# Ordering edits in a planned single-core kernel: state products a step later, PSUM exits by priority, two scan groups per output product, side splits spread out

## The chip, the cores and the metric

The kernel runs on one core of one Trainium2 chip, in one launch. The metric is device time in microseconds (us), the median of several runs; less is better. The engines are named as in the profile: PE is TensorE's matmul, PEld its weight load, DVE is VectorE, ACT is ScalarE, POOL is GpSimd, and SP is SyncE, which here issues nearly all DMAs.

## The reference

One step of a decoder layer in float32, on 1024 prompt tokens and on 8 samples of 8 tokens: a half-weight SwiGLU block, a token mixer of two branches, another half-weight SwiGLU block, and a final RMSNorm. Cut to what matters here:

```python
x = x + 0.5 * swiglu(rmsnorm(x, norm_ffn1), ffn1_w_in, ffn1_w_out)
proj = rmsnorm(x, norm_mix) @ w_in                       # u | z | xbc | dt | two gates
pool = (pool_mix(u) per group @ pool_w_group * pool_scale) @ pool_w_out
xbc  = silu(causal_conv(xbc));  xs, B, C = split(xbc)
per chunk of 128 tokens, per group of 8 heads (4 groups):
    st     = B^T (decay_end * dt * xs)                   # state product
    y      = (C B^T * decay) (dt * xs) + exp(a) * (C h)  # h: state before the chunk
    h      = h * chunk_decay + st
y    = rmsnorm_per_group((y + D * xs) * silu(z)) * ssd_norm
mix  = (gate0 * pool + gate1 * (y @ ssd_w_out)) @ w_o
x = x + mix
x = x + 0.5 * swiglu(rmsnorm(x, norm_ffn2), ffn2_w_in, ffn2_w_out)
return rmsnorm(x), and the new pooling, convolution and scan states
```

D_MODEL is 1024, D_FF 2816, the scan has 32 heads of 64 and a state of 128.

## The kernel before

All matrix products are made as three products of rounded float32 parts: a matrix is split into a high and a low part (`split`, `load_w`: ScalarE makes the high part, VectorE subtracts it), and high by high, low by high and high by low are summed in PSUM (`products`, L319 on). The products of the two feed-forward inputs and of `w_in` also use a Winograd-like scheme of seven products (`wino`). The tokens stand in two halves: half 0 has 512 prompt tokens, half 1 has 512 prompt tokens and the 64 sample tokens (576). An activation is held transposed, 128 channels by tokens, in a pool of 42 shared buffers (`act`); a product of half 0 fills one PSUM bank, one of half 1 two banks of 288 columns.

The stages follow each other: first feed-forward block, input projection (`in_proj`), mixer ("mix"), second feed-forward block. In the mixer the order of dense products is `pool_branch(0)`, `pool_branch(1)`, then for each half the products of `ssd_w_out` group by group (`ssd_out` for groups 0 to 2, `merge` for group 3 and the gates), then `out_proj`. Beside them the scan runs (`scan`, `ssd_group`): half 0, groups 0 to 3, then half 1; each group has 4 chunks (5 in half 1, the last being the samples).

The order is set by a planner in the kernel itself. `pe[0]` is TensorE time as the kernel counts it: each matmul adds its columns over 2400 us (four times that for plain float32). Side work is written as chains, generators that yield a pause in this time; `tick()`, which dense products call after each operand, steps every chain that is due, and `finish(c)` runs one to its end at once. So all pauses end at ticks. Afterwards the framework orders each engine's queue by the place in the program, with a model of its own of what is ready when; `tc.high_priority(n)` moves what stands in it n places ahead.

What the change touches:

- `ssd_group` (L1448 on): for each chunk the loads, a pause of `STEP[h]`, the second part of `ssd_a` (transposes `pxT`, `pcb`; `xdt`, `xd` and `btok` on VectorE and ScalarE; `ab`), a pause, `ssd_b` of the chunk before (`pyo`, `pyd`), then `ssd_st` of this chunk: the state product `pst<-xd,btok`, POOL's product of the old state and VectorE's sum (L1444).
- `gating` (L1482 on): y by z, the norm (`rstd`: `pss`, a power on POOL, then a pause of `R_WAIT0`, then `prb`), and the splits `yhl`, into buffers for two groups; it waits until the products of the group two before are counted in `freed`.
- `ssd_out`, `merge`, `out_proj`, `pool_branch`: the exits from PSUM on VectorE (L1565, L1593, L1609, L1252) have no priority.
- `load_w`: a weight block is loaded raw and split, unless it was split ahead by a side chain and written to DRAM (`part`, `parted`); then its two parts are loaded. `side()` splits ahead blocks of `ffn1_w_out`, `ffn2_w_in`, `w_o` and `pool_w_out` in the first stage, `split_so` those of `ssd_w_out` during `in_proj`. The pauses in `part` are `PART_W` (2.5) and `PART_PACE` (1.5).
- `in_proj` loads four pairs of `d` (`load_d`, high and low part of the pooled difference) ahead of the mixer; `pool_branch` loads the rest. `after1` starts the norm of half 1 (`norm_parts`) at pace 0.5.

Of the kernel before, what the change touches and what calls it, by code (L numbers as in the profile page):

```python
# [12 lines left out]
ALU = mybir.AluOpType  # L13

P = 128
D = 1024
KD = D // P
# [23 lines left out]

PRODUCTS = (("1", 0), ("2", 1), ("6", 0), ("5", 2), ("7", 0), ("3", 2), ("4", 0))

STEP = (5.4, 4.3)
STEP_S = 1.0
POST = 1.0
GP = (1.0, 1.2)
HN_AT, HN_PACE = 25.0, 2.0
MP = 2.0
R_WAIT0 = 2.0  # L50
R_WAIT = 0.5
F_Y = 0.5
X1_AT = 4.0
T_AT, T_PACE = 2.0, 1.5
TURN_AT, CONST_AT = 60.0, 40.0
HP, HP_ST = 40, 0
PART_AT, PART_W, PART_PACE = 6.0, 2.5, 1.5


@with_exitstack  # L60
def tile_hybrid_pool_ssd_macaron(
# [239 lines left out]

    parted, nth = {}, [0]

    def part(w, chunks):

        for k0, nk, c0 in chunks:
            t = fx(name="pr")[:, : nk * P]
            dma(t.rearrange("p (k c) -> p k c", c=P),
                w[k0 * P : (k0 + nk) * P, c0 : c0 + P].rearrange("(k p) c -> p k c", p=P))
            yield PART_W  # L310
            a = fx(F32R, "ph")[:, : nk * P]
            split(t, a, t.bitcast(F32R))
            to = [dp.tile([P, nk * P], F32, tag=nm("part"), name=nm("part")) for _ in range(2)]
            dma(to[0], a.bitcast(F32))
            dma(to[1], t)
            parted[w.tensor.name, k0, c0] = to
            yield PART_PACE

    def products(out, Wh, Wl, kk, cs, xs, k, nk):  # L319
        for ps_, (W, lo_) in enumerate(((Wh, False), (Wh, True), (Wl, False))):  # L320
# [490 lines left out]
    def after1(h, xt):  # L811
        o = []
        if h == 0:
            prep1m[0] = start(norm_parts(xt, 0, i_gm, o, HN_PACE, xnd), HN_AT), o
        for m in range(KD):
            dma(xspill[h][m], xt[m][:, : NTOK[h]])
        if h == 1:
            finish(prep1m[0][0])
            _, hi, lo, _, hl = prep1m[0][1][0]
            xn = [fx(name="xn") if k >= 4 else act((P, 576), name="xn") for k in range(KD)]  # L820
            for k in (0, 4, 1, 5, 2, 6, 3, 7):
                dma(xn[k][:, : NTOK[0]], xnd[k])
            prep1m[0][1][0] = (0, hi, lo, xn, hl)
            prep1m[1] = start(norm_parts(xt, 1, i_gm, o, 0.5), 0.5), o

    def mix_dt(h, xs):

# [299 lines left out]
    def in_proj(prep):  # L1127

        dts = []

        def plain(x):
            h = x[0]
            dts.append(mix_dt(h, [x]))
            for i in range(N_GATE[h]):
                pg = dense(W, 0, KD, OFF_G0 + i * P, [x], name="pg0")[0]
                t = fx(name="t0")
                func(t, pg, h, AF.Tanh, 0.5)
                dma(gd[h][i], t[:, : NTOK[h]])

        X = operands(prep, plain)  # L1140
        both = [(h, X[h]) for h in HALVES]
        last = [False]

        def worker():
            while work or not last[0]:
                if work:
                    yield from work.pop(0)
                else:
                    yield 1.0

        c = poster[0] = start(worker())
        work.append(sample_hist())
        split_so = start(part(ssd_w_out[0], so_chunks), 2.0)
        for i in range(N_GATE[0], 16, 2):
            proj_pair("g", i, i + 1, both)
        for g in range(NG):
            for kind, ia, ib in (("c", 16 + g, 20 + g), ("c", 4 * g, 4 * g + 1), ("c", 4 * g + 2, 4 * g + 3),
                                 ("u", 2 * g, 2 * g + 1), ("z", 4 * g, 4 * g + 1), ("z", 4 * g + 2, 4 * g + 3)):
                proj_pair(kind, ia, ib, both)
        ahead_d = []  # L1160
        for k in range(4):
            ahead_d.append(load_d(0, k))
        for i in range(N_GATE[1], N_GATE[0], 2):
            proj_pair("g", i, i + 1, both[1:])
        last[0] = True
        for c_ in dts + [split_so, c]:
            finish(c_)
        dma(new_pool_s[0, :, 0:7, :], state_pool[0, :, 8:HIST, :])
        return ahead_d
# [31 lines left out]
    def side():  # L1201
        yield from part(ffn1_w_out[0], out01)
        yield from part(ffn2_w_in[0], [(kb, 4, c0 + ff * P) for ff in range(N_PLAIN[0]) for kb in (0, 4) for c0 in (0, FF)])
        for w in (w_o[0], pool_w_out[0]):
            yield from part(w, [(kb, 4, m * P) for m in range(KD) for kb in (0, 4)])

    ffn(wi1, ffn1_w_out[0], prep1, after1, side=side())
    ahead_d = in_proj(prep1m)
# [17 lines left out]
    def pool_branch(h):  # L1226

        N = NTOK[h]
        fh, fl = [None] * KD, [None] * KD
        d = early[h]  # L1230

        def fetch_d(gi):
            for k in (2 * gi, 2 * gi + 1):
                if k not in d:
                    d[k] = load_d(h, k)

        fetch_d(0)
        for gi in range(4):
            if gi < 3:
                fetch_d(gi + 1)  # L1240
            dh, dl = zip(*(d.pop(k) for k in (2 * gi, 2 * gi + 1)))
            for j, pg in enumerate(dense2(wg[gi], 0, 0, [(h, dh, dl)], ("ps", "ps"), name="pgm")):
                m = gi * 2 + j
                fh[m], fl[m] = act((P, N), F32R, "fh"), act((P, N), F32R, "fl")
                for pt, (a, b) in zip(pg[0], PIECES[h]):
                    split(pt[:, : b - a], fh[m][:, a:b], fl[m][:, a:b], cols[:, i_ps + m : i_ps + m + 1])
        for m in range(KD):
            t = act((P, N), name="t0")
            dma(t, gd[h][m])
            pb = dense(pool_w_out[0], 0, KD, m * P, [(h, fh, fl)], name="pbp")[0]  # L1250
            for pt, (a, b) in zip(pb, PIECES[h]):
                V.scalar_tensor_tensor(t[:, a:b], t[:, a:b], 1.0, pt[:, : b - a], op0=ALU.add, op1=ALU.mult)  # L1252
            dma(accd[h][m], t)
            if h == 0 and m in (4, 6):
                early[1][m // 2 - 2] = load_d(1, m // 2 - 2)
# [192 lines left out]
    def ssd_group(h, g, Bf, Cf, xs4, dts, zs):  # L1448
        y4 = xs4
        prev = None  # L1450
        step = STEP[h]
        for c in range(4 + h):
            ga = ssd_a(h, g, c, Bf, Cf, xs4, dts)
            next(ga)
            if c == 3:
                for j in range(4):
                    z = act((P, NTOK[h]), name="z")
                    dma(z, zd[h][g * 4 + j])
                    zs.append(z)
            yield step  # L1460
            try:
                next(ga)
            except StopIteration as e:
                a = e.value
            yield step
            if prev:
                for w in ssd_b(h, g, *prev, Cf, y4, dts):
                    yield w
            prev = (c, a, ssd_st(h, g, c, a, dts))
        yield step  # L1470
        for w in ssd_b(h, g, *prev, Cf, y4, dts):
            yield w
        if h == 1:
            pt = psum("ps", "pfin")
# [76 lines left out]
        finish(gated[h, g][0])  # L1551
        return gated[h, g][1][0]

    def ssd_out(h, g, acc):

        yn = scanned(h, g)
        for m in range(KD):
            pb = dense(ssd_w_out[0], g * 4, 4, m * P, [yn], name="pso")[0]
            if g == 0:
                acc[m] = act((P, NTOK[h]), name="acc2")  # L1560
            for pt, (a, b) in zip(pb, PIECES[h]):
                if g == 0:
                    S.copy(acc[m][:, a:b], pt[:, : b - a])
                else:
                    V.tensor_tensor(acc[m][:, a:b], acc[m][:, a:b], pt[:, : b - a], op=ALU.add)  # L1565
        freed[0] += 1

    def merge(h, acc):

        N = NTOK[h]  # L1570
        t1 = [None] * KD
# [10 lines left out]
                merged[0] += 1  # L1582

        ch = start(head(), MP)
        yn = scanned(h, NG - 1)
        mh, ml = [], []
        for m in range(KD):
            pb = dense(ssd_w_out[0], (NG - 1) * 4, 4, m * P, [yn], name="pso")[0]
            while merged[0] <= m:
                ch.step()  # L1590
            a_, b_ = act((P, N), F32R, "mh"), act((P, N), F32R, "ml")
            for pt, (a, b) in zip(pb, PIECES[h]):
                V.scalar_tensor_tensor(t1[m][:, a:b], t1[m][:, a:b], 1.0, pt[:, : b - a], op0=ALU.add, op1=ALU.mult)  # L1593
            V.tensor_tensor(t1[m], t1[m], acc[m], op=ALU.add)
            split(t1[m], a_, b_, 0.5)
            mh.append(a_)
            ml.append(b_)
        freed[0] += 1
        return mh, ml

    def out_proj(h, mh, ml):
        N = NTOK[h]
        out = []
        for m in range(KD):
            x_ = act((P, N), name="x2")
            dma(x_, xspill[h][m])
            pw = dense(w_o[0], 0, KD, m * P, [(h, mh, ml)], name="pwo")[0]
            for pt, (a, b) in zip(pw, PIECES[h]):
                V.tensor_tensor(x_[:, a:b], x_[:, a:b], pt[:, : b - a], op=ALU.add)  # L1609
            dma(xspill[h][m], x_)  # L1610
            if h == 1:
                out.append(x_)
# [4 lines left out]
        pool_branch(h)  # L1617
    for h in HALVES:
        acc = [None] * KD
        for g in range(NG - 1):  # L1620
            ssd_out(h, g, acc)
        mhl = merge(h, acc)
        if h == 1:
            o = []
            prep2.append((start(norm_parts(reload(0), 0, i_g2, o, 2.0)), o))
# [126 lines left out]
```

## Time and profile before

| | |
|---|---|
| median of 3 runs | 2969.01 us (2965.47 to 2973.89) |
| the profiled execution's own time | 2975.98 us |
| its span, first to last instruction | 2974.2 us |
| mean granted TensorE clock | 0.987 |
| PE busy | 2838.9 us (95%) |
| PEld busy | 2579.6 us (87%) |
| DVE busy | 1763.4 us (59%) |
| ACT busy | 1374.6 us (46%) |
| POOL busy | 989.6 us (33%) |
| DMA moved | 528.96 MB |

How to read it: the profile is one execution. A row of waits says which engine stood before which tile's instruction, what ended it, and then the total in us, how often, and the longest. A window row gives its length, the busy time of PE, PEld, DVE, ACT and POOL with their instructions, the granted TensorE clock, the DMA share and GB/s. An order-of-time row begins with start and duration in us; what stands in brackets is the idle time before it and what ended that. Matmuls are pipelined and their rows overlap: the distance of two starts is what one costs.

### The profile page before, as it was taken

How to read it: one execution, taken by the hardware profiler on the slowest of the kernel's cores; microseconds unless marked ns; L12 is line 12 of the kernel's file. 1: busy time of each engine (PE TensorE's matmuls, PEld its weight loads, DVE VectorE, ACT ScalarE, POOL GpSimd, SP SyncE). 2: the span in 40 equal slices, each digit the busy share in tenths (PEclk: the TensorE clock that was granted, in tenths of full speed). 3: DMA queues.
4: the chain of work that ended last, by engine and by line, in shares of the span. 5: the costliest groups of instructions: out<-in, count | busy, mean ns of one | idle time of the engine just before them, and what ended most of it. 6: DMA issues, size and time to landing. Idle time of an engine off the chain costs nothing. (4 is left out here: it accounts for less than half of the span.)

```text
span 2974.2 us, 51139 instructions
## 1 busy us (share of the span) xinstructions
PE 2838.9 (95%) x18494; PEld 2579.6 (87%) x18494; DVE 1763.4 (59%) x2843; ACT 1374.6 (46%) x3008; POOL 989.6 (33%) x1011
## 2 busy tenths in 40 slices
PE   7999999999999989999989999889999999999998
PEld 6999899789989989998977887678888999997898
DVE  6665655534375696877865657766665544453432
ACT  5444444423345555554545555566333444443422
POOL 5444444100133454555522223322234444440000
PEclk9999999999999999999999999999999999999999
DMA  4677663856346663333368777776765422226652
GB/s 124 199 238 234 200 202 114 270 182 207 111 123 218 217 204 102 125 96 125 104 205 295 259 265 228 256 220 204 234 234 176 150 79 82 84 96 210 210 162 72
DMA packets 535709, 528.96 MB, mean 178 GB/s; under 512 B 38164, under 2 KB 367752, under 8 KB 535448
## 3 DMA queue, kind: packets, MB, share of 16 engines
q1 hardware_dynamic: 535440, 525.70, 55.5%
q8 instruction: 145, 2.38, 0.3%
q14 instruction: 108, 0.88, 0.1%
q10 hardware_dynamic: 16, 0.00, 0.0%
HBM read 374.36 MB, written 151.44 MB: 177 GB/s over the span
## 5 line engine op out<-in xcount | busy, mean ns | idle before, releaser
L162 PE MATMUL pw<-X,wh 128*128 128x288 f32 (+1 forms) x2484 | 623.4, 330 | 11.0 <-ACT v L559 3.5
L162 PE MATMUL pw<-X,wl 128*128 128x288 f32 (+1 forms) x1644 | 472.7, 288 | 4.6 <-DVE wl L443 4.6
L162 PEld LDWEIGHTS pw<-X,wh 128*128 128x128 f32 x2484 | 418.2, 189 | 49.9 <-ACT v L559 4.1
L162 PE MATMUL pw<-hl,wh 128*128 128x512 f32 x1072 | 391.9, 399 | 9.0 <-DVE t L563 5.2
L162 PE MATMUL pw<-hi,wh 128*128 128x288 f32 x1120 | 332.9, 297 | 4.8 <-ACT t L595 3.6
L162 PE MATMUL pw<-lo,wh 128*128 128x288 f32 x1120 | 331.5, 296 | 0.0
L162 PE MATMUL pw<-hi,wl 128*128 128x288 f32 x1120 | 331.4, 296 | 0.0
L443 DVE TENSOR_TENSOR wl<-s,wh 128x512 fp32r<-128x512 f32 x288 | 220.6, 768 | 179.4 <-ACT wh L442 154.6
L436 POOL TENSOR_TENSOR s<-wraw,wraw 128x512 f32<-128x512 f32 x144 | 204.4, 1420 | 338.3 <-DVE wl L443 226.3
L162 PEld LDWEIGHTS pw<-X,wl 128*128 128x128 f32 x1644 | 310.8, 189 | 5.5 <-DVE wl L443 5.5
L162 PE MATMUL pw<-hl,wl 128*128 128x256 f32 x1072 | 300.2, 280 | 1.9 <-DVE wl L443 1.8
L294 DVE TENSOR_TENSOR wl<-wraw,wh 128x512 fp32r<-128x512 f32 x196 | 136.3, 696 | 246.0 <-ACT wh L293 231.2
L293 ACT ACTIVATE wh<-wraw 128x512 fp32r<-128x512 f32 x196 | 117.8, 603 | 299.5 <-PE po L162 224.5
L162 PEld LDWEIGHTS pw<-hl,wh 128*128 128x128 f32 x1072 | 201.8, 188 | 46.9 <-DVE t L563 6.6
L443 DVE TENSOR_TENSOR wl<-wraw,wh 128x512 fp32r<-128x512 f32 x216 | 169.7, 786 | 121.1 <-ACT wh L442 114.0
L442 ACT ACTIVATE wh<-s 128x512 fp32r<-128x512 f32 x288 | 181.2, 629 | 124.8 <-PE pw L162 121.1
L162 PEld LDWEIGHTS pw<-hi,wh 128*128 128x128 f32 x1120 | 211.7, 189 | 17.7 <-ACT t L595 4.3
L162 PE MATMUL po<-hh,wh 128*128 128x288 f32 (+1 forms) x800 | 211.3, 324 | 4.4 <-ACT hh L354 4.3
L162 PEld LDWEIGHTS pw<-lo,wh 128*128 128x128 f32 x1120 | 211.9, 189 | 0.0
L162 PEld LDWEIGHTS pw<-hi,wl 128*128 128x128 f32 x1120 | 211.9, 189 | 0.0
L162 PE MATMUL po<-hr,wh 128*128 128x288 f32 (+1 forms) x800 | 211.5, 323 | 0.2 <-DVE hr L356 0.2
L162 PE MATMUL po<-hh,wl 128*128 128x288 f32 (+1 forms) x800 | 211.1, 323 | 0.0
(384 smaller groups left out, 6371.8 us busy)
## 6 DMA issues: line engine op xcount, KB each, us to landing
wraw<-in_ffn_w_in_dram SPq DMA_DIRECT2D x188, 256.0 KB
wh<-part SPq DMA_DIRECT2D x188, 256.0 KB
wl<-part SPq DMA_DIRECT2D x188, 256.0 KB
wraw<-in_w_in_dram SPq DMA_DIRECT2D x144, 256.0 KB
wraw<-in_ffn_w_out_dram SPq DMA_DIRECT2D x120, 256.0 KB
part<-ph SPq DMA_DIRECT2D x96, 256.0 KB
part<-pr SPq DMA_DIRECT2D x96, 256.0 KB
ab<-acsd SPq DMA_DIRECT2D x64, 256.0 KB
```

What stands on the lines that cost most here:

```text
L162: T.matmul(out, lhsT, rhs, start=start, stop=stop, skip_group_check=free)
L293: S.activation(wh, raw, AF.Copy)
L294: V.tensor_tensor(wl, raw, wh.bitcast(F32), op=ALU.subtract)
L436: G.tensor_tensor(t, a, b, op=op)
L442: S.activation(wh, a, AF.Copy)
L443: V.tensor_tensor(wl, a, wh.bitcast(F32), op=ALU.subtract)
```

## The change

It does nine things. (1) `ssd_st` of a chunk is called in the next chunk's round, between the two pauses, and after the last pause for the last chunk. (2) `in_proj` loads six pairs of `d` ahead. (3) `R_WAIT0` is 3.5. (4) In half 1 the scan's groups 0 and 1 go into one output product of eight operands (`SETS`), and `freed` counts both at its end. (5) Five exits from PSUM get `high_priority(60)`. (6) `pool_w_out` is no longer split ahead. (7) The side splits start later and pause longer: 20 at first, then 4.0 and 3.0; for `ssd_w_out` 5.0 and 5.0. (8) The norm of half 1 before `in_proj` has pace 1.2. (9) `STEP` is 5.2 and 4.1.

```diff
@@ -41,20 +41,21 @@
 
 PRODUCTS = (("1", 0), ("2", 1), ("6", 0), ("5", 2), ("7", 0), ("3", 2), ("4", 0))
 
-STEP = (5.4, 4.3)
+STEP = (5.2, 4.1)
 STEP_S = 1.0
 POST = 1.0
 GP = (1.0, 1.2)
 HN_AT, HN_PACE = 25.0, 2.0
 MP = 2.0
-R_WAIT0 = 2.0
+R_WAIT0 = 3.5
 R_WAIT = 0.5
 F_Y = 0.5
 X1_AT = 4.0
 T_AT, T_PACE = 2.0, 1.5
 TURN_AT, CONST_AT = 60.0, 40.0
-HP, HP_ST = 40, 0
-PART_AT, PART_W, PART_PACE = 6.0, 2.5, 1.5
+HP, HP_ST, HP_EV = 40, 0, 60
+SETS = (((0,), (1,), (2,), (3,)), ((0, 1), (2,), (3,)))
+PART_AT, PART_W, PART_PACE = 20.0, 4.0, 3.0
 
 
 @with_exitstack
@@ -301,20 +302,20 @@
 
     parted, nth = {}, [0]
 
-    def part(w, chunks):
+    def part(w, chunks, wait=PART_W, pace=PART_PACE):
 
         for k0, nk, c0 in chunks:
             t = fx(name="pr")[:, : nk * P]
             dma(t.rearrange("p (k c) -> p k c", c=P),
                 w[k0 * P : (k0 + nk) * P, c0 : c0 + P].rearrange("(k p) c -> p k c", p=P))
-            yield PART_W
+            yield wait
             a = fx(F32R, "ph")[:, : nk * P]
             split(t, a, t.bitcast(F32R))
             to = [dp.tile([P, nk * P], F32, tag=nm("part"), name=nm("part")) for _ in range(2)]
             dma(to[0], a.bitcast(F32))
             dma(to[1], t)
             parted[w.tensor.name, k0, c0] = to
-            yield PART_PACE
+            yield pace
 
     def products(out, Wh, Wl, kk, cs, xs, k, nk):
         for ps_, (W, lo_) in enumerate(((Wh, False), (Wh, True), (Wl, False))):
@@ -821,7 +822,7 @@
             for k in (0, 4, 1, 5, 2, 6, 3, 7):
                 dma(xn[k][:, : NTOK[0]], xnd[k])
             prep1m[0][1][0] = (0, hi, lo, xn, hl)
-            prep1m[1] = start(norm_parts(xt, 1, i_gm, o, 0.5), 0.5), o
+            prep1m[1] = start(norm_parts(xt, 1, i_gm, o, 1.2), 0.5), o
 
     def mix_dt(h, xs):
 
@@ -1150,7 +1151,7 @@
 
         c = poster[0] = start(worker())
         work.append(sample_hist())
-        split_so = start(part(ssd_w_out[0], so_chunks), 2.0)
+        split_so = start(part(ssd_w_out[0], so_chunks, 5.0, 5.0), 2.0)
         for i in range(N_GATE[0], 16, 2):
             proj_pair("g", i, i + 1, both)
         for g in range(NG):
@@ -1158,7 +1159,7 @@
                                  ("u", 2 * g, 2 * g + 1), ("z", 4 * g, 4 * g + 1), ("z", 4 * g + 2, 4 * g + 3)):
                 proj_pair(kind, ia, ib, both)
         ahead_d = []
-        for k in range(4):
+        for k in range(6):
             ahead_d.append(load_d(0, k))
         for i in range(N_GATE[1], N_GATE[0], 2):
             proj_pair("g", i, i + 1, both[1:])
@@ -1201,8 +1202,7 @@
     def side():
         yield from part(ffn1_w_out[0], out01)
         yield from part(ffn2_w_in[0], [(kb, 4, c0 + ff * P) for ff in range(N_PLAIN[0]) for kb in (0, 4) for c0 in (0, FF)])
-        for w in (w_o[0], pool_w_out[0]):
-            yield from part(w, [(kb, 4, m * P) for m in range(KD) for kb in (0, 4)])
+        yield from part(w_o[0], [(kb, 4, m * P) for m in range(KD) for kb in (0, 4)])
 
     ffn(wi1, ffn1_w_out[0], prep1, after1, side=side())
     ahead_d = in_proj(prep1m)
@@ -1248,8 +1248,9 @@
             t = act((P, N), name="t0")
             dma(t, gd[h][m])
             pb = dense(pool_w_out[0], 0, KD, m * P, [(h, fh, fl)], name="pbp")[0]
-            for pt, (a, b) in zip(pb, PIECES[h]):
-                V.scalar_tensor_tensor(t[:, a:b], t[:, a:b], 1.0, pt[:, : b - a], op0=ALU.add, op1=ALU.mult)
+            with tc.high_priority(HP_EV):
+                for pt, (a, b) in zip(pb, PIECES[h]):
+                    V.scalar_tensor_tensor(t[:, a:b], t[:, a:b], 1.0, pt[:, : b - a], op0=ALU.add, op1=ALU.mult)
             dma(accd[h][m], t)
             if h == 0 and m in (4, 6):
                 early[1][m // 2 - 2] = load_d(1, m // 2 - 2)
@@ -1458,6 +1459,8 @@
                     dma(z, zd[h][g * 4 + j])
                     zs.append(z)
             yield step
+            if prev:
+                prev += (ssd_st(h, g, *prev, dts),)
             try:
                 next(ga)
             except StopIteration as e:
@@ -1466,9 +1469,9 @@
             if prev:
                 for w in ssd_b(h, g, *prev, Cf, y4, dts):
                     yield w
-            prev = (c, a, ssd_st(h, g, c, a, dts))
+            prev = (c, a)
         yield step
-        for w in ssd_b(h, g, *prev, Cf, y4, dts):
+        for w in ssd_b(h, g, *prev, ssd_st(h, g, *prev, dts), Cf, y4, dts):
             yield w
         if h == 1:
             pt = psum("ps", "pfin")
@@ -1551,21 +1554,26 @@
         finish(gated[h, g][0])
         return gated[h, g][1][0]
 
-    def ssd_out(h, g, acc):
-
-        yn = scanned(h, g)
+    def ynorm(h, gs):
+        ys = [scanned(h, g) for g in gs]
+        return h, sum((y[1] for y in ys), []), sum((y[2] for y in ys), [])
+
+    def ssd_out(h, gs, acc):
+
+        yn = ynorm(h, gs)
         for m in range(KD):
-            pb = dense(ssd_w_out[0], g * 4, 4, m * P, [yn], name="pso")[0]
-            if g == 0:
+            pb = dense(ssd_w_out[0], gs[0] * 4, 4 * len(gs), m * P, [yn], name="pso")[0]
+            if gs[0] == 0:
                 acc[m] = act((P, NTOK[h]), name="acc2")
-            for pt, (a, b) in zip(pb, PIECES[h]):
-                if g == 0:
-                    S.copy(acc[m][:, a:b], pt[:, : b - a])
-                else:
-                    V.tensor_tensor(acc[m][:, a:b], acc[m][:, a:b], pt[:, : b - a], op=ALU.add)
-        freed[0] += 1
-
-    def merge(h, acc):
+            with tc.high_priority(HP_EV):
+                for pt, (a, b) in zip(pb, PIECES[h]):
+                    if gs[0] == 0:
+                        S.copy(acc[m][:, a:b], pt[:, : b - a])
+                    else:
+                        V.tensor_tensor(acc[m][:, a:b], acc[m][:, a:b], pt[:, : b - a], op=ALU.add)
+        freed[0] += len(gs)
+
+    def merge(h, gs, acc):
 
         N = NTOK[h]
         t1 = [None] * KD
@@ -1582,20 +1590,21 @@
                 merged[0] += 1
 
         ch = start(head(), MP)
-        yn = scanned(h, NG - 1)
+        yn = ynorm(h, gs)
         mh, ml = [], []
         for m in range(KD):
-            pb = dense(ssd_w_out[0], (NG - 1) * 4, 4, m * P, [yn], name="pso")[0]
+            pb = dense(ssd_w_out[0], gs[0] * 4, 4 * len(gs), m * P, [yn], name="pso")[0]
             while merged[0] <= m:
                 ch.step()
             a_, b_ = act((P, N), F32R, "mh"), act((P, N), F32R, "ml")
-            for pt, (a, b) in zip(pb, PIECES[h]):
-                V.scalar_tensor_tensor(t1[m][:, a:b], t1[m][:, a:b], 1.0, pt[:, : b - a], op0=ALU.add, op1=ALU.mult)
+            with tc.high_priority(HP_EV):
+                for pt, (a, b) in zip(pb, PIECES[h]):
+                    V.scalar_tensor_tensor(t1[m][:, a:b], t1[m][:, a:b], 1.0, pt[:, : b - a], op0=ALU.add, op1=ALU.mult)
             V.tensor_tensor(t1[m], t1[m], acc[m], op=ALU.add)
             split(t1[m], a_, b_, 0.5)
             mh.append(a_)
             ml.append(b_)
-        freed[0] += 1
+        freed[0] += len(gs)
         return mh, ml
 
     def out_proj(h, mh, ml):
@@ -1605,8 +1614,9 @@
             x_ = act((P, N), name="x2")
             dma(x_, xspill[h][m])
             pw = dense(w_o[0], 0, KD, m * P, [(h, mh, ml)], name="pwo")[0]
-            for pt, (a, b) in zip(pw, PIECES[h]):
-                V.tensor_tensor(x_[:, a:b], x_[:, a:b], pt[:, : b - a], op=ALU.add)
+            with tc.high_priority(HP_EV):
+                for pt, (a, b) in zip(pw, PIECES[h]):
+                    V.tensor_tensor(x_[:, a:b], x_[:, a:b], pt[:, : b - a], op=ALU.add)
             dma(xspill[h][m], x_)
             if h == 1:
                 out.append(x_)
@@ -1617,9 +1627,9 @@
         pool_branch(h)
     for h in HALVES:
         acc = [None] * KD
-        for g in range(NG - 1):
-            ssd_out(h, g, acc)
-        mhl = merge(h, acc)
+        for gs in SETS[h][:-1]:
+            ssd_out(h, gs, acc)
+        mhl = merge(h, SETS[h][-1], acc)
         if h == 1:
             o = []
             prep2.append((start(norm_parts(reload(0), 0, i_g2, o, 2.0)), o))
```

## The prediction

> **What bounds the kernel.** I read the page's first part, then the waits of TensorE over the whole span, then the windows around its longest waits, then the order of time on TensorE, VectorE and SyncE there.
>
> ```profile
> span 2974.2 us, 51139 instructions
> ...
> PE 2838.9 (95%) x18494; PEld 2579.6 (87%) x18494; DVE 1763.4 (59%) x2843; ACT 1374.6 (46%) x3008; POOL 989.6 (33%) x1011
> ```
>
> TensorE is busy 2838.9 of 2974.2 us, so 135 us is all that better order can win; the change alters no matmul, only when each is asked for. The execution's own time is 2975.98 us, 1.8 us beside the span and 7 us over the median of the runs (2969.01). I sum savings against this execution and take them off the median.
>
> The waits of TensorE (total us, times, longest us):
>
> ```profile
> PE pst L162 <- DVE xd L1333: 8.1, 4, 5.4
> PE pgm L162 <- DMA d<-dl: 7.8, 1, 7.8
> ...
> PE pw L162 <- DVE t L563: 5.2, 6, 1.6
> PE pg L162 <- DVE wl L294: 4.9, 3, 2.5
> ...
> PE prb L166 <- POOL rsm L362: 4.2, 4, 1.6
> ...
> PE pst L162 <- ACT ab L1343: 3.6, 2, 2.7
> ...
> PE pso L162 <- DVE t L1593: 2.6, 4, 1.1
> PE pso L162 <- DVE acc L1565: 2.3, 2, 1.5
> ...
> PE pbp L162 <- DMA wl<-part: 2.0, 2, 1.1
> PE pwo L162 <- DVE x L1609: 1.9, 1, 1.9
> ```
>
> No wait is large; the change aims at these ten rows, 42.6 us together. A wait also costs afterwards. In windows around three of them the granted clock (the column after POOL's) is low:
>
> ```profile
> 1550.00:1567.00 17.00, 9.17 (x32) 6.96 (x31) 1.70 (x3) 1.38 (x2) 0.64 (x1) 0.70 0.96 339
> 1872.00:1884.00 12.00, 6.55 (x17) 4.28 (x16) 11.20 (x16) 9.01 (x22) 8.01 (x5) 0.72 1.00 339
> 826.00:834.00 8.00, 5.67 (x18) 4.49 (x19) 8.00 (x12) 4.89 (x9) 3.29 (x5) 0.79 0.26 66
> ```
>
> (1-0.70)x17 = 5.1, (1-0.72)x12 = 3.4 and (1-0.79)x8 = 1.7 us of clock are missing, part of it while TensorE stands anyway. The third window's longest wait is 2.5 us, so short waits cost clock too. The Trainium skill, TensorE: Matmul & The Clock Gate, Part 1 (The HAM clock gate), has the clock fall to half after an idle window of about 3.4 us and rise after as long a busy one. By that rule only the waits of 7.8 and 5.4 us would cost clock, and the sum below would lack 1.7 us; the 0.79 row disagrees.
>
> **Term 1: state products a step later.** `pst` of a chunk is now asked for one planner step later, just before the next chunk's transposes; its input `xd` is by then done. Its two matmuls, its exit by VectorE and POOL's product with the old state stay, one step later in their queues too. The longest case, on TensorE and on VectorE:
>
> ```profile
> 1872.92 0.39 PE L162 MATMUL pwo<-ml,wh 128*128 128x512 f32 x1
> 1873.15 0.39 PE L162 MATMUL pwo<-mh,wl 128*128 128x512 f32 x1
> 1878.98 2.04 PE L162 MATMUL pst<-xd,btok 128*128 128x512 f32 x2 [5.45 <-DVE xd L1333]
> 1880.04 1.42 PE L162 MATMUL pwo<-mh,wh 128*128 128x512 f32 x1
> ```
> ```profile
> 1876.48 1.16 DVE L358 SCALAR_TENSOR_TENSOR ml<-t,mh 128x512 fp32r<-128x512 f32 x1
> ```
>
> What is late next is seen here: the `pwo` products before the wait are those of the first four of merge's splits, in order, and the fifth `ml` ends within 1876.48+1.16 = 1877.6. Without `pst` TensorE would still stand until about then; of 5.45 us some 1.4 goes for certain. The other `pst` waits, 8.1+3.6-5.45 = 6.3 us, are short and have ready products behind them; I take 4. With 0.6 of clock: 6 us. Bounds: 1 (all of them become waits for merge and `pyd`) to 11.7+2 = 13.7. Against it stands one more step of life for `xd` in the 42 shared buffers.
>
> **Term 2: six instead of four pairs of `d` ahead.** TensorE's wait, and SyncE's issues:
>
> ```profile
> 1560.59 0.79 PE L162 MATMUL pgm<-d,wh 128*128 128x512 f32 x1 [7.83 <-DMA d<-dl]
> ```
> ```profile
> 1544.87 0.40 SPq L1175 DMA_DIRECT2D d<-dh  x1
> 1547.22 0.32 SPq L1517 DMA_DIRECT2D dts<-dtp  x1
> ...
> 1555.19 0.32 SPq L1175 DMA_DIRECT2D d<-dl  x1
> 1556.53 0.32 SPq L1175 DMA_DIRECT2D d<-dl  x1
> ...
> 1559.88 0.32 SPq L1175 DMA_DIRECT2D d<-dl  x1
> ```
>
> The `dl` of pair 4 stands behind 13 loads of the scan (1547.22 to 1555.19) and ends the wait of 7.8 us at 1560.6, 5.4 us after its issue. Pairs 4 and 5 now go with the early ones, before the scan's loads. Late next are pairs 6 and 7, whose last issue at 1559.88 moves up only by the four issues that left, 4x0.67 = 2.7 us, so lands near 1557.2+5.4 = 1562.6. Between stand 24 products of pair 4/5, some 24x0.23 = 5.5 us by the starts of the `pwo` rows above, from 1560.6-7.8 = 1552.8. So about 4 us of waiting is left, 3.8 goes, with 1.2 of clock: 5 us. Bounds: 0 (SyncE holds the weights of the last gate pair behind the four loads) to 7.8+3 = 10.8.
>
> **Term 3: longer waits behind POOL's power.** `R_WAIT0` 2.0 to 3.5 lets `prb` be asked for later: 1.5 of 4.2 us, because where a finish is forced (the last group of a half) the pause is skipped. Bounds: -1 to 4.2.
>
> **Term 4: two groups in one product in half 1.** Sixteen exits of VectorE and the waits for them go, but the first product now needs group 1 of the scan, too. The exits as a group (busy us, mean ns, idle before), and `yhl` by tile (ns min, median and max, first and last start):
>
> ```profile
> L1565 DVE TENSOR_TENSOR acc<-acc,pso 128x288 f32<-128x288 f32 x26 | 10.8, 447 | 5.1 <-PE pso L162 5.0
> ```
> ```profile
> L162 PE MATMUL pso<-yhl,wh x444: 288/295/696, 1960.2 to 2129.8; 128*128 128x288 f32 x148
> ...
> L354 ACT ACTIVATE yhl<-xs,cols x12: 757/763/780, 1977.4 to 2119.7; 128x576 fp32r<-128x576 f32 x12
> ```
>
> 16x0.447 = 7.2 us of VectorE is hidden work; its 2.3 us of waits go. The products began at 1960.2, while group 1's first split began at 1977.4. The forced finish brings that forward, and two output blocks of four operands from group 0 cover it: 48 products of 288 columns at 288/512 of those 0.23, that is 48x0.13 = 6.2 us, beside scan work. I take 3.3 us of new waiting: -1 net. Bounds: -10 (the splits then come one per 0.76+0.81 us and TensorE takes 6x0.13 = 0.78 for each) to +4. Group 2's splits wait for buffers of group 0, which come free with 7x0.78 us of products left: nothing.
>
> **Term 5: exits by priority.** They overtake VectorE's scan work in a queue order that is fixed beforehand. Waits 2.6+1.9 us; I take 3 and 0.5 of clock: 3.5. Bounds: -4 (the overtaken scan work, as in term 1, is waited for) to 6.
>
> **Term 6: `pool_w_out` split on the spot.** Sixteen side splits go from the first stage; thirty-two come into the pool branch:
>
> ```profile
> L294 DVE TENSOR_TENSOR wl<-wraw,wh 128x512 fp32r<-128x512 f32 x196 | 136.3, 696 | 246.0 <-ACT wh L293 231.2
> L293 ACT ACTIVATE wh<-wraw 128x512 fp32r<-128x512 f32 x196 | 117.8, 603 | 299.5 <-PE po L162 224.5
> ```
> ```profile
> 1600.00:1650.00 50.00, 45.07 (x272) 37.21 (x270) 29.47 (x49) 27.89 (x68) 12.63 (x10) 0.97 0.87 302
> 1650.00:1726.00 76.00, 75.61 (x592) 69.96 (x591) 48.56 (x85) 41.13 (x106) 22.98 (x19) 1.00 0.81 271
> ```
>
> 32x0.696 = 22 us of VectorE and 32x0.603 = 19 us of ScalarE lie on some 155 us in which they are 59 to 64% and 54 to 56% busy: VectorE goes to about 75%. One load in place of two relieves DMA, 81 to 87% busy, and the 2.0 us of `wl<-part` go; I take 3 us of waits for splits: -1. Bounds: -20 to +2; the cover is three buffers ahead, 3x12x0.23 = 8.3 us.
>
> **Term 7: side splits spread.** Pacing before (first and last issue of the two batches), the window of the second batch, and its waits:
>
> ```profile
> L314 SPq DMA_DIRECT2D part<-ph x56: 319/339/811, 112.7 to 461.8; - x56
> ```
> ```profile
> L314 SPq DMA_DIRECT2D part<-ph x32: 319/339/497, 897.1 to 1093.5; - x32
> ```
> ```profile
> 1000.00:1100.00 100.00, 95.33 (x628) 87.85 (x628) 88.79 (x136) 59.39 (x120) 55.25 (x69) 1.00 0.64 205
> ```
> ```profile
> PE pw L162 <- ACT wh L442: 3.2, 1, 3.2
> PE pw L162 <- DVE wl L443: 3.1, 2, 2.4
> PE pst L166 <- DVE ra L1097: 1.6, 3, 0.9
> ```
>
> A chunk took (461.8-112.7)/55 = 6.35 us and the planner moves only after a product, at 1.28 or 1.44: 2.5 and 1.5 were two such ticks each. 4.0 and 3.0 are three each, so 9.5 us a chunk: forty end near 510, before the stage's end. The 32 chunks of `ssd_w_out` (5.0 and 5.0, four ticks each, 12.7 us) end near 1300 instead of 1093. At 1000 to 1110 VectorE is 89% busy and TensorE waits 3.2+3.1+1.6 = 7.9 us: 4 goes, and 1 comes later. In the first stage 2 of the 5.2 us behind L563 go with fewer splits. Together 5 us. Bounds: -4 (busier from 1110 to 1300) to 13.
>
> **Term 8: `norm_parts` at pace 1.2.** The 4.9 us of `pg` lie where VectorE is busy 8.00 of 8 us (window 826); half the pace relieves it: 2 and 1 of clock: 3. It ends well inside the seven plain products of half 0. Bounds: -3 to 6.6.
>
> **Term 9: scan step 5.2 and 4.1.** The planner moves in ticks of 3x512/2400 = 0.64 or 3x576/2400 = 0.72. 5.4 and 5.2 are both nine or eight ticks, 4.3 and 4.1 both seven or six. So nothing, unless another chain's work falls between. Bounds: -2 to 2.
>
> Sum: 6+5+1.5-1+3.5-1+5+3+0 = 22 us; 2969-22 = 2947.
>
> **Rivals.** (a) The waits move on: VectorE's lag, the merge chain and SyncE's issue rate stay, and terms 1, 2 and 7 come back under other names. For it: `ml` at 1877.6 and pairs 6 and 7. Against: in 1650 to 1726 the scan ran beside dense products with VectorE at 64% and TensorE at 75.61 of 76 us. 22-16 = 6 us: 2963. (b) Slower: the splits of `pool_w_out` come too late. The place is the pool branch, the price that of the row of `pg` behind L294, 4.9/3 = 1.6 us a chunk; it decides once VectorE lags more than the 8.3 us of cover. With three quarters of 32 chunks late, 24x1.6 = 38 us in place of term 6's -1: 2969-23+38 = 2984. For it: that row, same operation; against: in that window VectorE was busy without a gap.
>
> **How the numbers follow.** A measurement of this kernel can tell about 0.3%, 8.9 us, from no change. Forecast 0.68, all of it faster, its own range 2918 to 2959 (the terms' bounds partly together); rival (a) 0.18, within 0.3%; rival (b) 0.14, slower. The range 2916 to 2975 takes in the forecast and (a) and leaves out most of (b).
>
> **What would show it.** Right: no `pst` wait over 1 us; the `pgm` wait at most half; `acc` and L1593 waits gone; 16 fewer L1565 rows; few waits at 1000 to 1110; the scan's `pfin` at the same places among the products. Wrong: many `pbp` waits behind L294 (rival b), or `pwo`, `pyd` and `pgm` waits as large as before (rival a), or a wait of over 10 us at half 1's first `pso`.

## The result, and the profile after

| | before | after | ratio, 95% interval |
|---|---|---|---|
| median of 4 runs each | 2968.82 us (2965.47 to 2973.89) | 2942.99 us (2942.58 to 2943.95) | 0.9912 [0.9895, 0.9929] |
| repeated on another chip | 2968.16 us (10 runs) | 2941.07 us (4 runs) | 0.9906 [0.9892, 0.9919] |
| forecast | | 2947 us, range 2916 to 2975 | |

The change won 26 to 27 us; 22 were forecast. The page of the profile after begins:

```profile
span 2942.2 us, 51070 instructions
...
PE 2836.7 (96%) x18494; PEld 2575.2 (88%) x18494; DVE 1779.3 (60%) x2843; ACT 1385.2 (47%) x3024; POOL 1001.0 (34%) x1011
```

The profiled execution took 2943.95 us. Against the one before, the span is 32.0 us shorter and TensorE's busy time 2.2 us. So 29.8 us of the 32.0 are idle time that went (135.3 to 105.5 us). ScalarE has 16 instructions more: the side splits of `pool_w_out` went (16 fewer) and 32 on the spot came.

The waits of TensorE after, the rows that answer to those of before:

```profile
PE pgm L163 <- DVE fl L359: 3.7, 1, 3.7
...
PE pwo L163 <- DVE ml L359: 2.6, 2, 2.3
...
PE pso L163 <- DVE t L1602: 2.2, 2, 1.9
...
PE pacs L163 <- DVE dt L868: 2.1, 1, 2.1
...
PE pwo L163 <- DVE x L1619: 1.9, 2, 1.6
...
PE pg L163 <- DVE wl L295: 0.8, 2, 0.5
...
PE prb L167 <- POOL rsm L363: 0.7, 1, 0.7
...
PE pw L163 <- DVE t L564: 0.7, 1, 0.7
```

Lines have moved by one to ten. Gone are the `pst` waits of the scan (11.7 us), the `pgm` wait for `d` (7.8), those of `pso` for `acc` on VectorE (2.3) and of `pbp` for `wl` by DMA (2.0). Reduced are `pg` (4.9 to 0.8), `prb` (4.2 to 0.7) and `pw` behind VectorE's `t` in the first stage (5.2 to 0.7). Hardly changed are the waits for the exits of `merge` (L1593, now L1602: 2.6 to 2.2) and of `out_proj` (1.9). New are `pgm` behind `fl` (3.7), `pwo` behind `ml` (2.6) and `pacs` (2.1).

Cut at the first matmul of each stage's products in the order of time, the lengths and, in brackets, the waits of TensorE, each counted in the stage in which it ends, are (us; e1, e2, e3 and e8 are told below):

| stage | before | after | e1 | e2 | e3 | e8 |
|---|---|---|---|---|---|---|
| first block, input (to `po`) | 539.9 (33.8) | 527.0 (23.9) | 535.0 (32.2) | 527.5 (25.2) | 535.9 (31.9) | 527.2 (23.6) |
| first block, output (to `pdt`) | 266.3 | 265.7 | 267.3 | 267.5 | 265.5 | 265.3 |
| input projection (to `pgm`) | 736.2 (22.3) | 733.3 (19.2) | 733.5 (19.9) | 737.9 (23.0) | 736.1 (21.3) | 736.0 (19.1) |
| pool branch (to `pso`) | 184.5 (15.7) | 183.1 (11.6) | 182.3 (12.0) | 198.1 (23.7) | 198.2 (23.1) | 192.1 (19.6) |
| rest of the mixer (to `pg`) | 479.4 (36.9) | 473.6 (29.3) | 471.3 (29.7) | 474.4 (32.3) | 476.6 (33.1) | 472.4 (32.2) |
| second block, input (to `po`) | 479.7 (7.8) | 473.7 (4.1) | 478.4 (6.7) | 474.3 (3.6) | 478.6 (7.1) | 473.6 (4.1) |
| second block, output | 288.2 | 285.6 | 287.0 | 290.5 | 289.0 | 288.4 |

The largest part, 12.9 us, came in the first stage, and 6.0 us in the input of the second block, where the text of the change alters nothing: `part` is used there, too, and its default pauses changed. The mixer, where most edits are, gave 7.2 us in all.

### The profile page after: what moved, and what is told of

Its sections match the earlier page's. It is cut to its first block, busy times and chain, and to the rows that moved or that the text cites. A ratio compares the mean times of both kernels' runs of the same rounds, so it can differ in the third digit from the quotient of the medians.

```text
span 2942.2 us, 51070 instructions
## 1 busy us (share of the span) xinstructions
PE 2836.7 (96%) x18494; PEld 2575.2 (88%) x18494; DVE 1779.3 (60%) x2843; ACT 1385.2 (47%) x3024; POOL 1001.0 (34%) x1011
## 4 chain that ended last, share of the span: by engine, by line
PE 79%; DVE 9%; DMA 4%; ACT 4%; issue 2%; POOL 1%; SPq 1%; DVEq 0%; ACTq 0%; POOLq 0%
PE pw L163 42%; PE po L163 18%; PE pso L163 4%; PE pg L163 3%; PE pwo L163 2%; PE pbp L163 2%; PE pu L163 2%; DVE ct L937 1%; PE pyd L163 1%; DVE wl L444 1%; ACT ab L1344 1%; DMA t<-gd 1%; DVE us L952 1%; PE pst L163 1%; PE pyo L163 1%
## 5 line engine op out<-in xcount | busy, mean ns | idle before, releaser
L295 DVE TENSOR_TENSOR wl<-wraw,wh 128x512 fp32r<-128x512 f32 x228 | 163.6, 721 | 250.3 <-ACT wh L294 233.2
L294 ACT ACTIVATE wh<-wraw 128x512 fp32r<-128x512 f32 x228 | 137.7, 607 | 322.8 <-PE po L163 243.9
L444 DVE TENSOR_TENSOR wl<-wraw,wh 128x512 fp32r<-128x512 f32 x216 | 168.9, 782 | 135.5 <-ACT wh L443 127.9
```

What stands on the lines that cost most here:

```text
L294: S.activation(wh, raw, AF.Copy)
L295: V.tensor_tensor(wl, raw, wh.bitcast(F32), op=ALU.subtract)
L444: V.tensor_tensor(wl, a, wh.bitcast(F32), op=ALU.subtract)
```

## The experiments

The question was which edit is worth how much, and whether the total is a sum. In e1 and e4 to e9 one edit of the changed kernel is undone (in e9 two); e2 and e3 put parts of it into the kernel before. Ratios are to the kernel before on the same chip; the changed kernel has 0.9912 and 0.9906 there, and 2942 us between its two medians.

**e1_sides_fast: the pace of side splits undone.**

```diff
-PART_AT, PART_W, PART_PACE = 20.0, 4.0, 3.0
+PART_AT, PART_W, PART_PACE = 6.0, 2.5, 1.5
-        split_so = start(part(ssd_w_out[0], so_chunks, 5.0, 5.0), 2.0)
+        split_so = start(part(ssd_w_out[0], so_chunks), 2.0)
```

> The changed kernel with the side splits at the old pace (first pause 6, then 2.5 and 1.5 everywhere, for ssd_w_out too). Theory A (the pace is the main source: the trace shows the first stage 13 us shorter, the input projection 3 and the last stage 8.6): 15 to 25 us lost, about 2963 us, the first output product of the first stage back from 529 to about 540, most of the waits for L564 and the loads of x back. Theory B (term 7 as forecast): 5 us lost, 2948. Theory C (fewer splits, not their pace, made the first stage shorter): under 4 us lost, 2945.

2956.69 us, 0.9966 [0.9955, 0.9978]: some 15 us lost, theory A. The waits in the first stage (100 to 540 us) of e1, and of the changed kernel:

```profile
PE ptr L167 <- DMA xin<-in_x_prompt_dram: 4.7, 3, 2.1
PE pw L163 <- DVE t L564: 4.0, 4, 1.6
```
```profile
PE po L163 <- ACT hh L355: 1.9, 2, 1.1
PE pw L163 <- ACT v L560: 1.8, 1, 1.8
PE pw L163 <- ACT t L596: 1.3, 1, 1.3
PE pw L163 <- DVE t L564: 0.7, 1, 0.7
```

The windows from 100 to 320 us of the kernel before, after and e1 show what the pace does: DMA (last but one column) is less busy while x is loaded.

```profile
100.00:320.00 220.00, 213.27 (x1435) 199.88 (x1434) 133.41 (x224) 105.65 (x243) 88.44 (x83) 0.99 0.71 228
```
```profile
100.00:320.00 220.00, 219.78 (x1499) 207.12 (x1497) 127.66 (x223) 106.43 (x243) 95.88 (x89) 1.00 0.61 194
```
```profile
100.00:320.00 220.00, 213.44 (x1433) 199.74 (x1432) 131.83 (x222) 105.20 (x242) 88.83 (x84) 0.99 0.71 229
```

TensorE stood 6.7 us of these 220 before and 0.2 us after, with VectorE about as busy; 5.2 of the 6.7 us were `ptr` behind loads of x. The busier DMA, a share of 0.71, is not the only difference: SyncE also issues these loads later. The issues of e1, then of the changed kernel, for the load of x behind the longest of these waits (2.15 us, ended at 133.3 in e1):

```profile
125.41 0.38 SPq L315 DMA_DIRECT2D part<-ph  x1
125.90 0.41 SPq L316 DMA_DIRECT2D part<-pr  x1
126.36 2.14 SPq L787 DMA_DIRECT2D xspill<-xr  x3
128.54 0.87 SPq L778 DMA_DIRECT2D xin<-in_x_prompt_dram  x1
```
```profile
117.29 0.94 SPq L778 DMA_DIRECT2D xin<-in_x_prompt_dram  x2
```

In e1 the load stands behind two stores of split parts and goes out 4.8 us before the wait ends. In the changed kernel it is the second of two in a row, 14 us ahead of its `ptr` (132.0). Which of the two weighs more, the fuller DMA or the later issue, was not separated. By the stages, the pace is worth 8.0 us in the first stage and 4.7 in the second block, where a wait of 3.3 us for ScalarE's `t` goes; in the input projection, whose 89% busy VectorE the prediction pointed at, 0.2 us. The waits at 990 to 1110 did fall, from 8.4 us in e1 to 3.8, but about as many came back in the rest of that stage.

**e3_before_no_pool and e2_before_sides: the kernel before with `pool_w_out` split on the spot, alone and with the new pace.**

```diff
-        for w in (w_o[0], pool_w_out[0]):
-            yield from part(w, [(kb, 4, m * P) for m in range(KD) for kb in (0, 4)])
+        yield from part(w_o[0], [(kb, 4, m * P) for m in range(KD) for kb in (0, 4)])
```

> The kernel before without pool_w_out split ahead, the pace of the others as before. Theory A: the 40 chunks end early at the old pace, the first stage wins only what is behind the last 16, 3 us, and the mixer keeps its length: about 2966. Theory B (term 6): 1 us lost, 2970. Theory C: 10 to 15 us won, about 2956. Rival (b) of the prediction: 15 us lost in the pool branch, 2984.

> The kernel before with the new pace of side splits and without pool_w_out among them, nothing else. Theory A: 15 to 25 us won, about 2949 us, the mixer as long as before (664 us). Theory B: 5-1 = 4 us won, 2965. Theory C: as A, but then e3 alone has it.

e3: 2980.81 us, 1.0054 [1.0037, 1.0071], 14 us slower: near the 15 us expected by rival (b), and met by none of the theories. e2: 2967.57 us, 1.0005 [0.9994, 1.0017]: the new pace takes it back, and no more. Both pool branches are 198 us long. The waits in that of e3, then the windows of the pool branch before, in e3 and after:

```profile
PE pgm L162 <- DMA d<-dl: 9.6, 1, 9.6
PE pss L162 <- DVE ssq L379: 3.3, 2, 2.3
PE pbp L162 <- ACT wh L293: 2.3, 3, 0.9
PE pgm L162 <- ACT r L400: 2.2, 1, 2.2
```
```profile
1542.00:1727.00 185.00, 169.94 (x1093) 145.68 (x1094) 99.80 (x169) 94.33 (x233) 42.90 (x35) 0.96 0.86 289
```
```profile
1537.00:1736.00 199.00, 176.22 (x1094) 150.40 (x1095) 121.66 (x201) 110.74 (x266) 44.01 (x35) 0.93 0.71 227
```
```profile
1526.00:1709.00 183.00, 171.97 (x1122) 147.81 (x1123) 124.84 (x205) 110.55 (x266) 47.00 (x38) 0.97 0.77 247
```

The mechanism isn't that of rival (b), though. Only 2.7 us of `pbp` waits are for a split (2.3 for `wh`, 0.4 for `wl`), and the wait for `d` is 1.8 us longer than before. Most of the others are waits of other work for a VectorE and a ScalarE that are 22 and 16 us busier (term 6 counted 22 and 19). With 7.4 us more of waits, nearly as much again is missing in clock: (1-0.93)x199 = 13.9 us against (1-0.96)x185 = 7.4.

**e8_ahead4: four pairs of `d` ahead.**

```diff
-        for k in range(6):
+        for k in range(4):
             ahead_d.append(load_d(0, k))
```

> The changed kernel with four pairs of d ahead instead of six. Term 2 (half of the wait was to stay): 5 us lost, 2948. Theory D, from the trace after, where no pgm wait for d is left at all, and from the kernel before without pool_w_out, where it is 9.6 us: 8 to 12 us lost, 2951 to 2955, a pgm wait of 7 us or more back and the clock near 0.7 in the 17 us around it.

2955.12 us, 0.9957 [0.9944, 0.9969]: 13 us lost, theory D. In its pool branch, 9.0 us longer, the wait is back, and the granted clock is 0.70 from 1536 to 1553 us, around it:

```profile
PE pgm L163 <- DMA d<-dl: 9.6, 1, 9.6
```

In the changed kernel SyncE issues pairs 4 and 5 here, and pairs 6 and 7 after the scan's loads as forecast:

```profile
1506.54 0.38 SPq L1176 DMA_DIRECT2D d<-dh  x1
...
1507.96 0.39 SPq L1176 DMA_DIRECT2D d<-dl  x1
...
1539.39 0.32 SPq L1176 DMA_DIRECT2D d<-dh  x1
...
1541.42 0.32 SPq L1176 DMA_DIRECT2D d<-dl  x1
```

Yet no product waits for them. The products of pairs 0 to 5 follow each other from 1526.1 to 1534.3, then come products of `pool_w_out` and of the scan, and the first of pair 6 starts at 1545.0 without a wait. TensorE's only wait between is 2.2 us, for a load of the scan (`xs`).

**e5_st_early: state products in their own round.**

```diff
-            if prev:
-                prev += (ssd_st(h, g, *prev, dts),)
...
-            prev = (c, a)
+            prev = (c, a, ssd_st(h, g, c, a, dts))
...
```

> The changed kernel with the state product of a chunk asked for in its own round again, as before. Term 1: 6 us lost, about 2949 us, with waits of pst on xd of 5 to 12 us in all back. Rival (a) (the waits only change their name): under 2 us lost, 2945, the pst waits back and those of pwo for ml and of the scan's other products smaller by as much.

2939.86 us, 0.9909 [0.9896, 0.9923]: no loss that the intervals can show. Its waits in the mixer hold

```profile
PE pst L163 <- ACT ea L1342: 4.9, 2, 3.4
PE prb L167 <- POOL rsm L363: 3.7, 3, 2.3
PE pst L163 <- DVE xd L1334: 3.0, 2, 1.7
```

7.9 us of `pst` waits that the changed kernel has not, and the same time: TensorE is idle for 105.9 us of the whole span, in the changed kernel for 105.5. In exchange `pwo` waits for `ml` for 0.5 us instead of 2.6, and the 3.7 us of `pgm` behind `fl` are gone. The pool branch is 8.8 us longer than in the changed kernel and the rest of the mixer 12.2 us shorter: rival (a), for this edit. The row of `prb` is back, too, although `R_WAIT0` is 3.5 here: see e9.

**e7_no_prio: exits at priority 0.**

```diff
-HP, HP_ST, HP_EV = 40, 0, 60
+HP, HP_ST, HP_EV = 40, 0, 0
```

> The changed kernel with the exits from PSUM at priority 0. Term 5: 3.5 us lost, 2946.5, waits of pso for the line of merge's exits and of pwo for x larger. Rival (priority only reorders work that is waited for anyway): within 2 us of 2943.

2940.92 us, 0.9909 [0.9896, 0.9923]: no loss either. The wait that the priority was meant for is larger again (with it 2.2 us, and 3.5 in e12, the changed kernel once more):

```profile
PE pso L163 <- DVE t L1602: 6.4, 5, 2.1
```

TensorE is idle for 107.7 us of the span, in the two profiles with the priority for 105.5 and 110.2: the priority moves waits, and takes none that shows.

**e6_single_sets: one scan group per product in half 1.**

```diff
-SETS = (((0,), (1,), (2,), (3,)), ((0, 1), (2,), (3,)))
+SETS = (((0,), (1,), (2,), (3,)), ((0,), (1,), (2,), (3,)))
```

> The changed kernel with one scan group per output product in half 1, as before. Term 4 (the new wait at the first product costs a little more than the exits save): 1 us won, 2942, the waits for yhl at half 1's first products gone and those for acc back. Rival (the saved exits are worth more): 3 to 6 us lost, 2946 to 2949.

2950.31 us, 0.9940 [0.9926, 0.9953]: 8 us lost: the rival's direction, and more than its 3 to 6 us. The sixteen exits were saved as counted (groups in half 1's products, of after and of e6):

```profile
L1573 DVE TENSOR_TENSOR acc<-acc,pso 128x288 f32<-128x288 f32 x16 | 6.5, 449 | 3.7 <-PE pso L163 3.7
```
```profile
L1573 DVE TENSOR_TENSOR acc<-acc,pso 128x288 f32<-128x288 f32 x32 | 13.0, 448 | 5.2 <-PE pso L163 5.2
```

From the first `pso` of half 1 to its first `pwo` the changed kernel takes 184.2 us (1944.0 to 2128.2) and e6 192.0 (1942.0 to 2133.9), which is the loss. Most of it lies where half 1's products begin, the place at which the prediction put a new wait (windows of after, then of e6):

```profile
1942.00:1985.00 43.00, 34.99 (x247) 28.62 (x246) 35.01 (x50) 26.60 (x74) 14.34 (x13) 0.92 0.56 185
```
```profile
1942.00:1985.00 43.00, 31.14 (x200) 24.49 (x199) 33.33 (x49) 29.15 (x81) 12.98 (x11) 0.81 0.56 181
```

TensorE stands 8.0 us there with two groups and 11.9 us with one, and its clock is 0.92 against 0.81. The wait for `yhl` that was feared is 1.2 us in the changed kernel:

```profile
1953.51 0.54 PE L163 MATMUL pso<-yhl,wh 128*128 128x288 f32 x2 [1.15 <-ACT yhl L355]
```

Why two groups fill this stretch better wasn't settled. The waits of e6 there are one for a state's load (3.6 us) and the others for the scan's own steps on VectorE and ScalarE (`xd`, `xdt`, `hst`, `ea`), none of them for `acc`. So the rival's reason, the saved exits, is not shown.

**e4_step: the scan's pauses back.**

```diff
-STEP = (5.2, 4.1)
+STEP = (5.4, 4.3)
```

> The changed kernel with the scan's pauses back at 5.4 and 4.3. Term 9 (all pauses end at the same ticks): no change within 2 us, 2943. Rival (other chains' work falls between, pauses end a tick later here and there, and the scan ends later among the products): 4 us or more lost, 2947 or more, and pfin of the last group later than at 2072.5 us of the span.

2947.3 us, 0.9944 [0.9929, 0.9959]: 5 us lost by the medians, 10 by the ratios, but the runs leave it open. Three of the six are at 2943.7 to 2944.7 us, near the changed kernel, and three at 2949.9 to 2955.5. The profiled one is of the first three; its span is 2942.0 us, as long as the changed kernel's 2942.2. So no trace shows where time would be lost.

What the trace does show is another order. The first `pfin` of the last group (2077.0 us) stands 47.8 us ahead of the first `pwo` of half 1 (2124.8). In the changed kernel it stands 55.7 us ahead (2072.5 and 2128.2), in the kernel before 47.3. The shorter pauses do move the scan forward among the products, as the rival said. The planner's own count for the loads of the scan's last chunk, an estimate and no measurement, is 1783.3 with the old pauses and 1768.2 with the new ones. A pause is counted from before the matmuls that the chain's own step asks for. After the 0.75 of `pxT` and `pcb`, 0.75+7x0.64 = 5.23 ends a pause of 5.2, and not one of 5.4.

**e9_short_waits: `R_WAIT0` and the pace of `norm_parts` back.**

```diff
-R_WAIT0 = 3.5
+R_WAIT0 = 2.0
-            prep1m[1] = start(norm_parts(xt, 1, i_gm, o, 1.2), 0.5), o
+            prep1m[1] = start(norm_parts(xt, 1, i_gm, o, 0.5), 0.5), o
```

> The changed kernel with R_WAIT0 back at 2.0 and the norm of half 1 back at pace 0.5. Terms 3 and 8: 1.5+3 = 4.5 us lost, about 2947.5 us; the input projection 2 to 4 us longer than 733, waits of pg for L295 at its start and of prb for POOL back. Rival (the norm's exits collide elsewhere anyway): within 2 us of 2943.

2947.86 us, 0.9931 [0.9919, 0.9943]: 6 us lost, near what terms 3 and 8 say together. Term 8 is seen in the trace. The input projection is 736.6 us, 3.3 more, and the start of it (790 to 892) has its wait back:

```profile
PE pg L163 <- DVE wl L295: 3.9, 2, 2.5
```

Term 3 is not. `prb` waits for POOL for 0.7 us here, as in the changed kernel, though `R_WAIT0` is 2.0 again; in e5 and e11, with `R_WAIT0` at 3.5 and the state products in their old place, it waits for 3.7 and 3.6 us. What took most of this wait away was term 1's edit. Where the other 3 us of the loss lie isn't shown.

**e10_pool_in_proj and e11_pool_st_early: a better version?** `pool_w_out` split ahead again, but in the input projection; in e11 with the edit of e5, too.

```diff
-        split_so = start(part(ssd_w_out[0], so_chunks, 5.0, 5.0), 2.0)
+        def ahead_split():
+            yield from part(pool_w_out[0], [(kb, 4, m * P) for m in range(KD) for kb in (0, 4)], 4.0, 5.0)
+            yield from part(ssd_w_out[0], so_chunks, 4.0, 5.0)
+
+        split_so = start(ahead_split(), 2.0)
```

> The changed kernel with pool_w_out split ahead again, but during the input projection, ahead of ssd_w_out there (pauses 4.0 and 5.0, 48 chunks). Theory E (splitting on the spot costs 14 us in the pool branch, as in the kernel before without it): the pool branch falls from 183 to about 170, 8 to 14 us won, 2929 to 2935. Theory F (beside the early loads of d and the later state products the splits are hidden): the pool branch stays at 181 to 185, 2941 to 2945.

> As e10_pool_in_proj, and the state products in their own round as in e5_st_early, where the pool branch was 192 us and the rest of the mixer shorter. Theory E: the pool branch at about 178, the rest as in e5, 2926 to 2932. Theory F: as e5, 2938 to 2942.

> The changed kernel itself, for comparison on the same chip: 2943 us by every theory, 0.9912 of the kernel before.

e10: 2958.58 us, 0.9969 [0.9957, 0.9981]; e11: 2950.14 us, 0.9938 [0.9925, 0.995]; the changed kernel beside them (e12) 2941.07 us. Neither is better. The pool branch stays at 185.4 us (theory F), and the input projection gets 9.4 us longer, for 16 more chunks. What splits ahead save on VectorE comes back as waits for the loads of the split parts, two per block instead of one (the waits of e10's pool branch; its profiled execution, 2948.85 us, is the fastest of its six):

```profile
PE pbp L163 <- DMA wh<-part: 8.1, 1, 8.1
PE pbp L163 <- ACT fh L355: 2.8, 1, 2.8
PE pbp L163 <- DMA wl<-part: 2.0, 2, 1.8
```

No version beat the changed kernel: e5 and e7 equal it within their intervals.

## Why the prediction was right, and where its steps failed

The sum, 22 us, came near the measured 26, and its sign held for the reason given: idle time of TensorE went (29.8 of 32.0 us), not work. That the sum came so near is luck in good part, since the terms inside it were mostly mis-sized and their errors cancel. By undoing edits in the changed kernel (medians against 2942 us; an interval is some 4 us to either side):

| term | forecast | measured |
|---|---|---|
| 1 state products | +6 | -2 (e5) |
| 2 pairs of `d` | +5 | +13 (e8) |
| 3 and 8 waits and pace of norms | +4.5 | +6 (e9) |
| 4 two groups | -1 | +8 (e6) |
| 5 exits by priority | +3.5 | -1 (e7) |
| 6 `pool_w_out` on the spot | -1 | -14 alone on the kernel before (e3) |
| 7 pace of side splits | +5 | +15 (e1) |
| 9 scan step | 0 | +5, left open (e4) |

The measured column adds to 30 us, and without term 6 to 44; the whole change won 26, so the edits aren't independent. Term 6 was measured on the kernel before alone and was not undone by itself in the changed kernel. In e10, where the splits ahead stand in the input projection, they leave the pool branch no shorter (185.4 us against 183.1). Terms 2, 4 and 7 came out above their upper bounds (10.8, 4 and 13 us).

- Terms 1 and 5 failed where rival (a) said. The row of `ml` at 1877.6, quoted in term 1, had said that the next product was nearly as late, and `pwo` behind `ml` is now a wait of its own (2.6 us). A queue of VectorE that is late as a whole wasn't helped by another order of those who wait for it.
- Term 2 had the gain too small by its path. It let only the products of pairs 4 and 5 cover pairs 6 and 7, and counted 24 of them; the trace has 12 for two pairs (36 from 1526.1 to 1534.3 for pairs 0 to 5), by which some 7 us of waiting, not 4, would have been left. In fact none was: products of `pool_w_out` and the scan filled the time up to 1545.0. All of the wait went, and the clock around it.
- Term 3 named the wrong edit: most of the `prb` wait went with the state products (e5, e9), not with the longer pause.
- Term 4 priced the wait that the edit adds (1.2 us in the trace, 3.3 taken) and not what the coarser product is worth at that place; the reason for that worth is open.
- Term 6's cover argument was right, the splits are in time; but 22 us of VectorE work put into a stage cost other waits there, and with them clock.
- Term 7 looked for the gain where VectorE is busiest. It came where side traffic delayed the loads of x and in the second block, where the default pauses also act.
- Term 8 held: the `pg` wait went from 4.9 to 0.8 us, and e9 has it back.
- Term 9 took the pause to begin after the step's matmuls. So `pfin`, which was to stay at the same places among the products, moved 8 us ahead.

On the clock: the Trainium skill, TensorE: Matmul & The Clock Gate, Part 1 (The HAM clock gate), lets it fall after an idle window of about 3.4 us. In the changed kernel it fell behind a single wait of 1.80 us. Below are the product that ended this wait, the window of the wait and the one behind it, and then a window with a longer wait, 2.1 us (the `pacs` row above):

```profile
510.04 0.50 PE L163 MATMUL pw<-X,wh 128*128 128x512 f32 x1 [1.80 <-ACT v L560]
```
```profile
508.00:511.40 3.40, 1.60 (x9) 1.21 (x8) 1.54 (x2) 2.86 (x6) 2.71 (x3) 1.00 0.11 38
511.40:514.80 3.40, 3.40 (x12) 2.87 (x11) 3.40 (x5) 1.32 (x4) 1.43 (x2) 0.50 0.71 248
```
```profile
820.00:830.00 10.00, 7.10 (x33) 5.15 (x32) 10.00 (x16) 4.50 (x8) 6.61 (x5) 1.00 0.25 69
```

Behind the wait of 1.80 us the granted clock was 0.50 for 3.4 us, although TensorE was busy all that time; around the longer wait it stayed at 1.00. The trace does not agree with a threshold on a single wait. It bears out the prediction's choice to charge clock to short waits, too; what decides between two such waits, these runs do not show.

## What to carry to other kernels

Where the bound engine is 95% busy, undo edits one by one before believing a list of terms: here two of eight were worth nothing and two were worth about three times their estimate, and the sum hid it. Side traffic here did best spread over the whole stage that has room for it; the place where it hurt was found from the loads that TensorE waited for, the DMA share there and what SyncE issued ahead of them, not from the busiest engine. A wait that follows a late queue only changed its name here; a wait for a load issued too late went for good.

## What the runs showed of the hardware

The cost of short waits in clock was larger than expected. In e3, from 1596 to 1736 us, TensorE stood 10.4 us and none of the waits was over 2.3 us; the mean granted clock was 0.94. In the kernel before, from 1600 to 1727, it stood 5.3 us with the clock at 0.99. A single wait of 1.80 us was followed by 3.4 us at a granted clock of 0.50. In e1 a load of x stood behind stores of split parts in SyncE's queue and went out at 128.5 us, where the changed kernel issued it at 117.8.
